# Two convolution tiles lead a mixer's GEMMs, its gates are woven in behind, and two gate tiles stand at the scan's end

## The chip, the cores and the metric

The kernel runs on one core of a Trainium2 chip. The metric is the time of one execution on the device in microseconds, median over the runs. The engines are TensorE (PE: matmuls, and its weight loads), VectorE (DVE), ScalarE (ACT), GpSimd (POOL) and SyncE (SP), whose queue issues most of the transfers. All matmul results land in PSUM, of which the kernel uses eight banks of 128 x 512 fp32.

## The reference

512 tokens of width 1024 pass through two layers of a first kind and two of a second. Only the mixers of the first kind change. With h the normalised input:

```python
proj = h @ w_in[l]
(qa, ka, va, qd, kd, vd, beta_logit, decay_logit, z, gate_logit) = jnp.split(proj, offsets, axis=-1)
...
y_attn = grid_attention(qa, ka, va) @ w_o_attn[l]
qkv = jax.nn.silu(centred_depthwise_conv(jnp.concatenate([qd, kd, vd], axis=-1), dn_conv_w[l]))
...
o = bidir_gated_deltanet(qd, kd, vd, beta, g)
o = rmsnorm(o, dn_out_norm_g[l]) * jax.nn.silu(z)
y_dn = o @ w_o_dn[l]
gates = jax.nn.sigmoid(gate_logit).reshape(b, s, N_BRANCH, D_MODEL)
mixed = gates[:, :, 0] * y_attn + gates[:, :, 1] * y_dn
x = x + mixed @ w_out[l]
```

The delta net is a recurrence over chunks of 64 tokens, run in both directions; before its scan, a triangular system is solved per chunk. A feed-forward layer follows each mixer.

## The kernel before, in words

Activations lie feature by token, as tiles of 128 features x 512 tokens. Every operand of a GEMM is split into a high and a low part (`xh`, `xl` and, per weight tile, `wh`, `wl`), and three matmuls per pair of tiles give fp32 accuracy. `wload` (L390) loads a 256 KB piece of weights, ACT rounds it to `wh`, and DVE subtracts to give `wl`; a running sum `aid` sends some of these subtractions to POOL instead. `g_fm` (L414) makes one output tile of 128 features from 1024 inputs: 24 matmuls of 512 columns in two pieces of weights, then an `evac` function on the result. Its output takes one of three PSUM banks `pg`.

The norm's factor per token, `R`, is applied to the results of the GEMMs and not to their inputs. So GEMMs can start before the norm is known: `lead` (L177) runs the first 16 steps of a mixer's GEMM on the inputs while the norm is worked out, and `follow` (L195) later runs what is left of these generators, that is their `evac`. Every `evac` here waits for `R`.

The mixer (L1325) has four sorts of work.

- The **delta net's preparation** (`prepare`, L1280): the gates (`g_dn_gates`, L864: a GEMM of 32 columns, then softplus, cumulative sums on PE, a trip through DRAM of sixteen small transfers on SP), the q, k and v projections with their convolution (`g_dn_inputs`, L947, twice, once per group of four heads, six tiles each), and the decay factors (`g_dn_decay`). Beside them run the grid attention's inputs (`g_grid_inputs`, L772). The `evac` of a convolution tile (L956) is a chain: DVE multiplies by `R` into `pad`, ACT and DVE apply five taps into `cva`, ACT and DVE make the silu, PE transposes four times into a `pt` bank, ACT copies out and squares, DVE reduces. At the end `rsqrt` steps give `dnr`, and DVE scales `tmk` and `tmq`, the keys and queries that the solve takes.
- The **solve** (`g_dn_solve`, L1012), a row by row elimination on DVE for two groups.
- The **scan** (`g_dn_scan`, L1111) of the two groups, with the grid attention beside it.
- **Background tiles** (`g_tanh`, L1254): four silu gates `z`, eight branch gates `ga` for the attention, eight branch gates `gd` for the delta net. Each is 24 matmuls; its `evac` is a DVE step into `tha`, a tanh on ACT into `thz`, for `z` one more DVE step, and a store to DRAM.

The work is woven by rates: `weave` (L219) always advances the generator that is furthest behind, and `run` pulls the background at a rate `R1[...]` per unit of foreground. `need` (L172) runs what is left of a name. A manual dependency in `pe` (L240) holds each background matmul behind the foreground instruction `pin` places back in the list of the last ones. From the program order the tile framework makes each engine's instruction order; every engine then works through its own in order.

After the scan come the output GEMM of the attention (results in `pg`, its `evac` into `u`), the norm of the delta net's output (`g_dn_out`), its GEMM, and the residual.

Of the kernel before, what the change touches and what calls it, by code (L numbers as in the profile page):

```python
# [11 lines left out]
AF = mybir.ActivationFunctionType  # L12
ALU = mybir.AluOpType
AX = mybir.AxisListType
# [5 lines left out]
T = 512  # L20
D = 1024
NT = 4
# [84 lines left out]
class Net:  # L107
# [839 lines left out]
    def g_dn_inputs(self, l, pool, ip, g):  # L947

        w = self.I["w_in"][l]
        out = {}  # L950
        ms = self.t(self.sm, [128, 2, NT, 4], "dnms")
        for kind in range(3):
            dst = self.t(pool, [128, NT, 256], "tm" + "qkv"[kind], bufs=2)
            out["qkv"[kind]] = dst

            def evac(i, ps, kind=kind, dst=dst):  # L956
                ft = 4 * kind + 2 * g + i
                c = [self.cols[:, 64 + 60 * l + 12 * j + ft : 65 + 60 * l + 12 * j + ft] for j in range(5)]
                p = self.pad[self.npad % 2]
                self.npad += 1  # L960
                self.tt(p[:, 2 : T + 2], ps, self.R, ALU.mult)
                a = self.t(ip, [128, T], "cva")
                self.act(a, p[:, 2 : T + 2], AF.Copy, scale=c[2])
                for j in (0, 1, 3, 4):
                    self.stt(a, p[:, j : j + T], c[j], a, ALU.mult, ALU.add)
                th = self.t(ip, [128, T], "cvt")
                self.act(th, a, AF.Tanh, scale=0.5)
                self.stt(a, th, 1.0, a, ALU.add, ALU.mult)
                pt = self.t(self.pt, [128, T], "pt")
                for t in range(NT):  # L970
                    self.tr(pt[:, 128 * t : 128 * t + 128], a[:, 128 * t : 128 * t + 128])
                p3 = pt.rearrange("p (t n) -> p t n", t=NT)
                self.act(dst[:, :, 128 * i : 128 * i + 128], p3, AF.Copy, scale=0.5 if kind == 2 else 1.0)
                if kind < 2:
                    sq = self.t(ip, [128, T], "cvt")
                    self.act(sq, pt, AF.Square)
                    self.V.tensor_reduce(ms[:, kind, :, 2 * i : 2 * i + 2],
                                         sq.rearrange("p (t h d) -> p t h d", t=NT, h=2), AX.X, ALU.add)

            yield from self.g_fm(w, D, 768 + 512 * kind + 256 * g, 256, self.xh, self.xl, evac, 128)  # L980
# [291 lines left out]
    def delta_net(self, l, od, inputs, attention):  # L1272
# [5 lines left out]
        ip, icm = self.pool(f"dni{l}", bufs=4)  # L1278

        def prepare():  # L1280
            G = yield from self.g_dn_gates(l, pool, ep, ip)
            x0 = yield from self.g_dn_inputs(l, pool, ip, 0)
            x1, E0, E1 = yield from self.weave(
                (self.g_dn_inputs(l, pool, ip, 1), 1.0), (self.g_dn_decay(l, ep, 0, G), R1[0]),
                (self.g_dn_decay(l, ep, 1, G), R1[0]),
            )
            return G, (x0, x1), (E0, E1)
# [31 lines left out]
    def begin_mixer(self, l):  # L1319
        self.zd = self.t(self.dr, [128, 4, T], f"zd{l}")  # L1320
        z = self.tanh_tiles(self.I["w_in"][l], 2336, 4, lambda f: self.zd[:, f, :], True)
        self.push("z", *z[2:])
        return [(g, 8) for g in z[:2]]

    def mixer(self, l):  # L1325
# [12 lines left out]
        self.follow()  # L1338
        self.push("ga", *self.tanh_tiles(w, 2848, 8, lambda f: thd[:, f, :]))
        self.push("gd", *self.tanh_tiles(w, 2848 + 1024, 8, lambda f: thd[:, 8 + f, :]))  # L1340
# [8 lines left out]
        for name in ("z", "ga", "gd"):  # L1349
            self.need(name)  # L1350
        pool, cm = self.pool(f"mo{l}", bufs=2)
# [607 lines left out]
```

## Time and profile before

| | |
|---|---|
| median of 3 runs | 3095.34 us (3093.31 to 3095.86) |
| the profiled execution | 3096.09 us, span 3094.3 us |
| PE busy | 3011.5 us, 97% |
| DVE busy | 2221.3 us, 72% |
| ACT busy | 1502.0 us, 49% |
| POOL busy | 416.4 us, 13% |
| granted PE clock, mean | 0.988 |

The span runs from the first to the last instruction of one execution. The busy share of an engine is an average over stages; for the change the two mixers count, of which layer 0's fills the span up to about 450 us and layer 1's stands from about 905 to 1310 us. The granted clock is 1 at full speed (2.4 GHz) and 0.5 at half (1.2 GHz); a stretch with a value between has run part of its time at either. The duration of a matmul in the trace contains its pipeline, so how fast PE works is read from the starts of neighbouring matmuls.

### The profile page before, as it was taken

The page shows a single profiled execution, that of the slowest core. Times are in us where ns is not written, and L with a number is a line of the kernel's source. Part 1 is how long each engine was busy: PE and PEld are TensorE (multiplying, and loading weights), DVE is VectorE, ACT ScalarE, POOL GpSimd, SP SyncE. Part 2 cuts the span into 40 slices and gives each one's busy share as a digit, 9 for nine tenths or more (in the row PEclk, how much of TensorE's full clock was granted, in tenths as well). Part 3 has the DMA queues.
Part 4 walks back from the last instruction along what each step waited for, and adds up shares of the span by engine and source line. Part 5 has one row for each costly group of instructions (what it writes and reads, how often), then busy time and mean ns, then how long its engine had stood idle before and what let it go on. Part 6 is the DMA issues. An engine that isn't in the chain of part 4 may idle for free. (4 is left out here: it accounts for less than half of the span.)

```text
span 3094.3 us, 54458 instructions
## 1 busy us (share of the span) xinstructions
PE 3011.5 (97%) x20148; PEld 2540.6 (82%) x20148; DVE 2221.3 (72%) x4974; ACT 1502.0 (49%) x3043; POOL 416.4 (13%) x550
## 2 busy tenths in 40 slices
PE   8989999999999899999999999999999999999999
PEld 6877778888888777788888898888888898878977
DVE  5988776777448887777774466778686666788684
ACT  3544744444324456544443344366464453476463
POOL 2433300000014343100000000200100010200200
PEclk9999999999999999999999999999999999999999
DMA  4435125333343342253333454522435545422525
GB/s 146 115 90 146 43 88 175 96 99 96 125 129 89 106 120 85 68 167 107 98 98 123 136 140 131 143 75 73 123 113 186 158 118 150 121 66 67 162 87 183
DMA packets 403116, 359.02 MB, mean 116 GB/s; under 512 B 32867, under 2 KB 350307, under 8 KB 402851
## 3 DMA queue, kind: packets, MB, share of 16 engines
q1 hardware_dynamic: 396707, 335.62, 37.6%
q0 software_dynamic: 6144, 19.93, 1.8%
q8 instruction: 159, 2.61, 0.4%
q14 instruction: 106, 0.87, 0.1%
HBM read 293.98 MB, written 61.47 MB: 115 GB/s over the span
## 5 line engine op out<-in xcount | busy, mean ns | idle before, releaser
L260 ACT ACTIVATE wh<-st 128x512 fp32r<-128x512 f32 x844 | 528.2, 629 | 788.5 <-PE pg L238 633.4
L254 DVE TENSOR_TENSOR wl<-st,wh 128x512 fp32r<-128x512 f32 x766 | 539.0, 705 | 402.0 <-ACT wh L260 397.2
L238 PE MATMUL pg<-xh,wh 128*128 128x512 f32 (+1 forms) x1824 | 733.0, 402 | 3.6 <-ACT wh L260 2.2
L238 PE MATMUL pg<-xh,wl 128*128 128x512 f32 (+1 forms) x1824 | 719.9, 395 | 5.3 <-POOL wl L254 5.3
L238 PE MATMUL pg<-xl,wh 128*128 128x512 f32 (+1 forms) x1824 | 712.2, 395 | 0.0
L238 PEld LDWEIGHTS pg<-xl,wh 128*128 128x128 f32 (+1 forms) x1824 | 343.4, 188 | 73.8 <-issue 0.4
L238 PEld LDWEIGHTS pg<-xh,wl 128*128 128x128 f32 (+1 forms) x1824 | 344.2, 189 | 72.0 <-POOL wl L254 7.0
L238 PEld LDWEIGHTS pg<-xh,wh 128*128 128x128 f32 (+1 forms) x1824 | 344.2, 189 | 70.7 <-ACT wh L260 2.6
L238 PE MATMUL pg<-wl,xh 128*128 128x256 f32 x928 | 265.1, 287 | 0.4 <-DVE wl L254 0.4
L238 PE MATMUL pg<-wh,xh 128*128 128x256 f32 x928 | 262.6, 287 | 1.1 <-DVE oz L257 0.8
L238 PE MATMUL pg<-wh,xl 128*128 128x256 f32 x928 | 263.0, 285 | 0.0
L238 PEld LDWEIGHTS pg<-wh,xh 128*128 128x128 f32 x928 | 176.3, 192 | 6.2 <-DVE oz L257 1.0
L238 PEld LDWEIGHTS pg<-wl,xh 128*128 128x128 f32 x928 | 177.9, 192 | 3.9 <-DVE wl L254 0.8
L238 PEld LDWEIGHTS pg<-wh,xl 128*128 128x128 f32 x928 | 177.7, 192 | 1.2
L485 POOL DMA_DIRECT2D xd<-xn x40 | 21.8, 544 | 1049.5 <-DVE xn L257 927.5
L254 POOL TENSOR_TENSOR wl<-st,wh 128x512 fp32r<-128x512 f32 x78 | 123.1, 1584 | 267.5 <-ACT wh L260 234.4
L238 PE MATMUL pg<-hh,wl 128*128 128x512 f32 x352 | 137.0, 389 | 0.0
L238 PE MATMUL pg<-hh,wh 128*128 128x512 f32 x352 | 136.7, 389 | 0.0
L238 PE MATMUL pg<-hl,wh 128*128 128x512 f32 x352 | 135.7, 389 | 0.0
L260 ACT ACTIVATE p<-pa,anb 128x128 f32<-128x128 f32 (+1 forms) x224 | 115.6, 517 | 36.9 <-DVE anb L725 34.0
L257 DVE SCALAR_TENSOR_TENSOR u<-pad,cols,u 128x512 f32<-128x512 f32 x176 | 127.3, 746 | 0.7
L260 ACT ACTIVATE ph<-pt 128x128 fp32r<-128x128 f32 (+1 forms) x224 | 94.9, 426 | 65.9 <-PE pt L251 64.5
(509 smaller groups left out, 6276.2 us busy)
## 6 DMA issues: line engine op xcount, KB each, us to landing
st<-in_w_in_dram SPq DMA_DIRECT2D x400, 256.0 KB
st<-in_w_up_dram SPq DMA_DIRECT2D x176, 256.0 KB
st<-in_w_down_dram SPq DMA_DIRECT2D x88, 256.0 KB
st<-in_w_out_dram SPq DMA_DIRECT2D x64, 256.0 KB
xo<-xd SPq DMA_DIRECT2D x48, 256.0 KB
th<-thz SPq DMA_DIRECT2D x48, 256.0 KB
xd<-xn POOLq DMA_DIRECT2D x40, 256.0 KB, 4.0
thd<-thz SPq DMA_DIRECT2D x32, 256.0 KB
```

What stands on the lines that cost most here:

```text
L238: return self.pe(self.PE.matmul(out, lhsT, rhs, start=start, stop=stop, **kw))
L254: return (eng or self.V).tensor_tensor(out, a, b, op)
L257: return self.V.scalar_tensor_tensor(out, a, s, b, op0, op1)
L260: return self.S.activation(out, in_, f, **kw)
L485: self.nc.gpsimd.dma_start(self.xd[:, k, :], x)
```

## The change

The convolution tile becomes a function of its own, `g_conv`. The two GEMM tiles that `lead` runs ahead of the norm are now the two q tiles of the first group (`begin_mixer`), and all four `z` tiles go to the background. `follow`, which finishes the led tiles, moves into `delta_net`, behind the opening of the pools that the convolution needs. In `prepare` the gates no longer come first: they are woven with the remaining four tiles of the first group (`led=2` leaves out the two that led). Two of the eight `gd` tiles are not pushed with the others but behind the scan, with `pin` at -12, which lets them stand among the last twelve foreground matmuls.

```diff
@@ -944,40 +944,51 @@
         self.act(gt, p4, AF.Exp)
         return beta3, fac, kds3, eg3, gt
 
-    def g_dn_inputs(self, l, pool, ip, g):
+    def g_conv(self, l, kind, f, dst, ms):
+        def evac(_, ps):
+            ft = 4 * kind + f
+            c = [self.cols[:, 64 + 60 * l + 12 * j + ft : 65 + 60 * l + 12 * j + ft] for j in range(5)]
+            p = self.pad[self.npad % 2]
+            self.npad += 1
+            self.tt(p[:, 2 : T + 2], ps, self.R, ALU.mult)
+            a = self.t(self.conv_pool, [128, T], "cva")
+            self.act(a, p[:, 2 : T + 2], AF.Copy, scale=c[2])
+            for j in (0, 1, 3, 4):
+                self.stt(a, p[:, j : j + T], c[j], a, ALU.mult, ALU.add)
+            th = self.t(self.conv_pool, [128, T], "cvt")
+            self.act(th, a, AF.Tanh, scale=0.5)
+            self.stt(a, th, 1.0, a, ALU.add, ALU.mult)
+            pt = self.t(self.pt, [128, T], "pt")
+            for t in range(NT):
+                self.tr(pt[:, 128 * t : 128 * t + 128], a[:, 128 * t : 128 * t + 128])
+            p3 = pt.rearrange("p (t n) -> p t n", t=NT)
+            i = f % 2
+            self.act(dst()[:, :, 128 * i : 128 * i + 128], p3, AF.Copy, scale=0.5 if kind == 2 else 1.0)
+            if kind < 2:
+                sq = self.t(self.conv_pool, [128, T], "cvt")
+                self.act(sq, pt, AF.Square)
+                self.V.tensor_reduce(ms()[:, kind, :, 2 * i : 2 * i + 2],
+                                     sq.rearrange("p (t h d) -> p t h d", t=NT, h=2), AX.X, ALU.add)
 
         w = self.I["w_in"][l]
-        out = {}
-        ms = self.t(self.sm, [128, 2, NT, 4], "dnms")
+        return self.g_fm(w, D, 768 + 512 * kind + 128 * f, 128, self.xh, self.xl, evac, 128)
+    def dn_tiles(self, pool, g):
+        x = {k: self.t(pool, [128, NT, 256], "tm" + k, bufs=2) for k in "qkv"}
+        return x, self.t(self.sm, [128, 2, NT, 4], "dnms")
+    def g_dn_inputs(self, l, g, tiles, led=0):
+        out, ms = tiles
         for kind in range(3):
-            dst = self.t(pool, [128, NT, 256], "tm" + "qkv"[kind], bufs=2)
-            out["qkv"[kind]] = dst
-
-            def evac(i, ps, kind=kind, dst=dst):
...
-            yield from self.g_fm(w, D, 768 + 512 * kind + 256 * g, 256, self.xh, self.xl, evac, 128)
+            for i in range(2):
+                if 2 * kind + i >= led:
+                    yield from self.g_conv(l, kind, 2 * g + i, lambda kind=kind: out["qkv"[kind]], lambda: ms)
         v = self.small(32, "dnv", 2)
         self.V.tensor_scalar(v, ms.rearrange("p a t h -> p (a t h)"), 4 * EPS, None, ALU.add)
         r = self.small(32, "dnr", 2)
@@ -1276,12 +1287,16 @@
         pool, cm = self.pool(f"dn{l}", bufs=2)
         ep, ecm = self.pool(f"dne{l}", bufs=4, side="right")
         ip, icm = self.pool(f"dni{l}", bufs=4)
+        self.conv_pool = ip
+        self.conv_tiles = self.dn_tiles(pool, 0)
+        self.follow()
 
         def prepare():
-            G = yield from self.g_dn_gates(l, pool, ep, ip)
-            x0 = yield from self.g_dn_inputs(l, pool, ip, 0)
+            x0, G = yield from self.weave(
+                (self.g_dn_inputs(l, 0, self.conv_tiles, 2), 1.0), (self.g_dn_gates(l, pool, ep, ip), 0.8)
+            )
             x1, E0, E1 = yield from self.weave(
-                (self.g_dn_inputs(l, pool, ip, 1), 1.0), (self.g_dn_decay(l, ep, 0, G), R1[0]),
+                (self.g_dn_inputs(l, 1, self.dn_tiles(pool, 1)), 1.0), (self.g_dn_decay(l, ep, 0, G), R1[0]),
                 (self.g_dn_decay(l, ep, 1, G), R1[0]),
             )
             return G, (x0, x1), (E0, E1)
@@ -1318,9 +1333,9 @@
 
     def begin_mixer(self, l):
         self.zd = self.t(self.dr, [128, 4, T], f"zd{l}")
-        z = self.tanh_tiles(self.I["w_in"][l], 2336, 4, lambda f: self.zd[:, f, :], True)
-        self.push("z", *z[2:])
-        return [(g, 8) for g in z[:2]]
+        self.push("z", *self.tanh_tiles(self.I["w_in"][l], 2336, 4, lambda f: self.zd[:, f, :], True))
+        lead = lambda i: self.g_conv(l, 0, i, lambda: self.conv_tiles[0]["q"], lambda: self.conv_tiles[1])
+        return [(lead(i), 8) for i in range(2)]
 
     def mixer(self, l):
         self.last = deque(self.last, maxlen=LAG[0])
@@ -1335,9 +1350,9 @@
         gp, gcm = self.pool(f"mix{l}", bufs=2)
         self.gp = gp
         od = [self.t(gp, [128, 2, T], f"o{g}", bufs=1) for g in range(2)]
-        self.follow()
         self.push("ga", *self.tanh_tiles(w, 2848, 8, lambda f: thd[:, f, :]))
-        self.push("gd", *self.tanh_tiles(w, 2848 + 1024, 8, lambda f: thd[:, 8 + f, :]))
+        gd = self.tanh_tiles(w, 2848 + 1024, 8, lambda f: thd[:, 8 + f, :])
+        self.push("gd", *gd[:6])
 
         def gate(f, ps, dst):
             th = self.t(dp, [128, T], "th", bufs=4)
@@ -1348,6 +1363,11 @@
         oa, hcm = self.delta_net(l, od, inputs, lambda pool, hp: self.g_grid_attention(l, pool, hp, qd, kd, vd, ad))
         for name in ("z", "ga", "gd"):
             self.need(name)
+        self.push("gd", *gd[6:])
+        self.pin = -12
+        self.need("gd")
+        self.pin = 0
         pool, cm = self.pool(f"mo{l}", bufs=2)
         mx = self.f32r_tiles(pool, NK, "m")
         dp, dcm = self.pool(f"md{l}", bufs=2)
```

How this moves instructions shows at two places. The first is DVE in layer 0 from the moment `R` is there. `tha`, `thz` are a gate tile's steps, `sq` (here) the result of the gates' GEMM, `beta`, `dnx`, `spe`, `spz` the softplus chain behind it, `pad` and `cva` a convolution's steps. Before:

```order
L257 SCALAR_TENSOR_TENSOR tha_389<-pg_274,R_376 128x512
L254 TENSOR_TENSOR sq_522<-pg_427,R_376 32x512
L257 SCALAR_TENSOR_TENSOR thz_391<-thz_391,tha_389 128x512
L257 SCALAR_TENSOR_TENSOR tha_395<-pg_311,R_376 128x512
L257 SCALAR_TENSOR_TENSOR thz_397<-thz_397,tha_395 128x512
L254 TENSOR_TENSOR wl_714<-st_712,wh_713 128x512
L880 TENSOR_SCALAR beta_528<-beta_528 128x64
L254 TENSOR_TENSOR dnx_531<-pa_420,r_dn_dt_bias_416 128x64
```

After the change the first eight rows, in front of these, are `pad` of the two led tiles (from `pg_274` and `pg_311`) and six of their taps:

```order
L257 SCALAR_TENSOR_TENSOR cva_403<-pad_5_98,cols_104,cva_403 128x512
L254 TENSOR_TENSOR wl_653<-st_651,wh_652 128x512
L257 SCALAR_TENSOR_TENSOR cva_422<-pad_6_99,cols_104,cva_422 128x512
L254 TENSOR_TENSOR pad_5_98<-pg_440,R_376 128x512
L257 SCALAR_TENSOR_TENSOR cva_403<-cvt_409,cva_403 128x512
L257 SCALAR_TENSOR_TENSOR cva_623<-pad_5_98,cols_104,cva_623 128x512 x4
L973 TENSOR_REDUCE dnms_401<-cvt_418 128x4x2
L257 SCALAR_TENSOR_TENSOR cva_422<-cvt_428,cva_422 128x512
L254 TENSOR_TENSOR sq_687<-pg_537,R_376 32x512
```

Before, the two silu tiles and the gates stand first, and the first `pad` comes seventeen rows behind the first row here; after the change two convolutions stand first, then a third, and the gates' `sq` comes sixteen rows behind the first.

The second is PE at the end of layer 0's scan. `po` is the grid attention's output, `qf`, `S`, `wt`, `qk`, `y` are operands of the scan, `ph` and `pl` next to weights are the attention's result as the input of the output GEMM, whose first tile is `pg_5459`; `xh` and `xl` are the mixer's input. Before:

```order
L238 MATMUL po_4628<-ph_4705,v_4152 128x256
L238 MATMUL po_4628<-pl_4706,v_4152 64x256
L238 MATMUL pg_5459<-ph_4861,wh_5461 128x512
L238 MATMUL pg_5459<-ph_4861,wl_5462 128x512
L238 MATMUL pg_5459<-pl_4863,wh_5461 128x512
```

After the change the first kept gate tile, `pg_5333`, begins among the scan's last products:

```order
L238 MATMUL pt_5230<-qk_2026,y_1002_5231 64x64 x4
L238 MATMUL pt_5229<-qk_2026,y_1002_5231 64x64 x4
L238 MATMUL pa_5248<-S_997_5192,wt_987_5112 64x64 x4
L238 MATMUL pg_5333<-xh_28_160,wh_5335 128x512
L238 MATMUL pg_5333<-xh_28_160,wl_5336 128x512
L238 MATMUL pg_5333<-xl_36_168,wh_5335 128x512
L238 MATMUL pg_5333<-xh_29_161,wh_5335 128x512
L238 MATMUL pa_5249<-qf_984_5092,S_997_5192 64x64 x4
L238 MATMUL pg_5333<-xh_29_161,wl_5336 128x512
```

and the second, `pg_5375`, ends right ahead of the output GEMM:

```order
L238 MATMUL pg_5375<-xl_42_174,wh_5395 128x512
L238 MATMUL pg_5375<-xh_35_167,wh_5395 128x512
L238 MATMUL pg_5375<-xh_35_167,wl_5396 128x512
L238 MATMUL pg_5375<-xl_43_175,wh_5395 128x512
L238 MATMUL pg_5459<-ph_4777,wh_5461 128x512
L238 MATMUL pg_5459<-ph_4777,wl_5462 128x512
```

Before, the output GEMM follows the last product of the attention at once; after the change 48 matmuls of the two kept tiles stand between, the first 16 of them woven with products of the scan.

## Rows read from the trace of the kernel before

**Rows 1.** The page, part 1: busy time, share of the span, instructions.
```profile
span 3094.3 us, 54458 instructions
...
PE 3011.5 (97%) x20148; PEld 2540.6 (82%) x20148; DVE 2221.3 (72%) x4974; ACT 1502.0 (49%) x3043; POOL 416.4 (13%) x550
```

**Rows 2.** Busy time by stretch, layer 0 and then layer 1, from R on.
```profile
core 0: us, PE busy (x) PEld busy (x) DVE busy (x) ACT busy (x) POOL busy (x), PEclk, DMA share, GB/s
45.60:60.00 14.40, 13.74 (x77) 12.32 (x78) 10.99 (x25) 4.04 (x8) 2.59 (x2) 0.88 0.30 92
60.00:75.00 15.00, 15.00 (x126) 12.51 (x125) 7.77 (x15) 4.92 (x9) 1.72 (x1) 0.89 0.23 58
75.00:185.00 110.00, 108.22 (x613) 89.46 (x610) 102.85 (x200) 53.44 (x96) 53.48 (x44) 1.00 0.37 102
185.00:200.60 15.60, 8.84 (x41) 7.50 (x42) 14.41 (x28) 8.69 (x16) 4.40 (x6) 0.67 0.38 125
sum 155.00, PE 145.79 PEld 121.80 DVE 136.01 ACT 71.09 POOL 62.18; mean PE 36.45 PEld 30.45 DVE 34.00 ACT 17.77 POOL 15.54
...
920.00:937.00 17.00, 17.00 (x154) 14.59 (x153) 9.76 (x19) 4.51 (x10) 1.29 (x1) 0.90 0.26 67
937.00:1052.00 115.00, 110.96 (x608) 91.68 (x606) 102.44 (x202) 56.33 (x99) 52.47 (x45) 1.00 0.37 102
...
sum 160.00, PE 150.00 PEld 125.01 DVE 134.32 ACT 72.90 POOL 59.94; mean PE 37.50 PEld 31.25 DVE 33.58 ACT 18.23 POOL 14.98
```

**Rows 3.** Groups of DVE instructions by form, 45.6 to 200.6 us.
```profile
L257 DVE SCALAR_TENSOR_TENSOR cva<-pad,cols,cva 128x512 f32<-128x512 f32 x48 | 39.8, 832 | 2.2 <-ACT cva L260 1.6
L254 DVE TENSOR_TENSOR wl<-st,wh 128x512 fp32r<-128x512 f32 x22 | 17.1, 782 | 3.8 <-ACT wh L260 3.7
...
L257 DVE SCALAR_TENSOR_TENSOR thz<-thz,tha 128x512 f32<-128x512 f32 x4 | 3.8, 958 | 0.8 <-ACT thz L260 0.7
...
L257 DVE SCALAR_TENSOR_TENSOR tha<-pg,R 128x512 f32<-128x512 f32 x4 | 2.8, 688 | 2.0 <-ACT R L260 1.7 <-PE pg L238 0.2
```

**Rows 4.** PE in order of time, both preparations' ends: start, duration, instruction, [idle before].
```profile
189.18 1.09 PE L251 MATMUL pt<-c_ident,cva 128*128 128x128 f32 x4 [4.89 <-DVE hl L254]
192.85 1.09 PE L251 MATMUL pt<-c_ident,cva 128*128 128x128 f32 x4 [2.59 <-DVE dnv L982]
...
1055.38 1.09 PE L251 MATMUL pt<-c_ident,cva 128*128 128x128 f32 x4 [4.73 <-DVE hl L254]
1059.05 1.09 PE L251 MATMUL pt<-c_ident,cva 128*128 128x128 f32 x4 [2.58 <-DVE dnv L982]
```

**Rows 5.** PE in order of time at the scan's end, both layers.
```profile
433.11 0.79 PE L238 MATMUL pg<-ph,wh 128*128 128x512 f32 x1 [3.90 <-ACT ph L260]
433.70 0.63 PE L238 MATMUL pg<-ph,wl 128*128 128x512 f32 x1
434.13 0.63 PE L238 MATMUL pg<-pl,wh 128*128 128x512 f32 x1
...
446.22 0.40 PE L238 MATMUL pg<-ph,wl 128*128 128x512 f32 x1
446.45 0.40 PE L238 MATMUL pg<-pl,wh 128*128 128x512 f32 x1
...
1297.23 0.80 PE L238 MATMUL pg<-ph,wh 128*128 128x512 f32 x1 [3.79 <-ACT ph L260]
```

**Rows 6.** Busy time by stretch, after the scan in layer 0 (columns as rows 2).
```profile
433.10:446.00 12.90, 12.89 (x54) 10.82 (x55) 5.61 (x21) 3.63 (x6) 0.53 (x1) 0.64 0.73 224
```

**Rows 7.** GpSimd and DVE in order of time, layer 0; then page, part 5.
```profile
170.13 3.79 POOL L254 TENSOR_TENSOR wl<-st,wh 128x512 fp32r<-128x512 f32 x2 [6.62 <-ACT wh L260]
...
170.82 1.29 DVE L254 TENSOR_TENSOR nw<-nwb 128x16 f32<-128x16 f32 x1
...
L257 DVE SCALAR_TENSOR_TENSOR u<-pad,cols,u 128x512 f32<-128x512 f32 x176 | 127.3, 746 | 0.7
```

More of the change, by code (lines that the diff above doesn't have):

```diff
@@ L945, in g_dn_gates @@
         return beta3, fac, kds3, eg3, gt
-    def g_dn_inputs(self, l, pool, ip, g):
-        w = self.I["w_in"][l]
-        out = {}
-        ms = self.t(self.sm, [128, 2, NT, 4], "dnms")
-        for kind in range(3):
-            dst = self.t(pool, [128, NT, 256], "tm" + "qkv"[kind], bufs=2)
-            out["qkv"[kind]] = dst
-            def evac(i, ps, kind=kind, dst=dst):
[L957 to L978, printed above, removed]
-            yield from self.g_fm(w, D, 768 + 512 * kind + 256 * g, 256, self.xh, self.xl, evac, 128)
```

## The prediction

> **What bounds the kernel now.** The page's first part [rows 1] comes first: TensorE (PE) is busy 3011.5 of 3094.3 us, so a change that adds and removes no matmul can only win PE's idle time, about 83 us, and what is lost while its clock is granted at half. The page's slices put most of that idle time outside the start into the two mixers, so I cut the first half of each mixer into stretches [rows 2]: from the moment R is ready (45.6 us in layer 0, 906.9 us in layer 1) to the end of the scaled q and k tiles that the solve needs (200.6 and 1066.9 us). I call that the preparation; it takes 155.0 and 160.0 us. VectorE (DVE) is busy 136.0 us of the first and 134.3 us of the second, PE 145.8 and 150.0 us. So both are nearly full, and not at the same time: early on DVE is starved (busy for 7.8 of 15.0 us from 60 to 75 us, for 9.8 of 17.0 us from 920 to 937 us) while PE works; in the middle both run; at the end DVE is full (14.4 of 15.6 us) and PE works for only 8.8 of 15.6 us.
>
> The end is where it shows on PE [rows 4]: the transposes of the last convolution tiles wait 4.89 and 2.59 us in layer 0, 4.73 us and again 2.6 us in layer 1. The releasers are DVE instructions: a queue of convolution steps comes due when no matmul is left to cover it.
>
> The second place is the scan's end [rows 5]: PE stands 3.90 us (layer 0) and 3.79 us (layer 1) before the first matmul of the attention's output GEMM, and that GEMM then starts at the lower clock: neighbouring matmuls begin 0.43 us apart (433.70, 434.13) where they are 0.23 us apart later (446.22, 446.45). The granted clock from 433.1 to 446.0 us is 0.64 on average [rows 6].
>
> **What moves.** The two silu-gate tiles that led each mixer's GEMMs (24 matmuls of 512 columns each) become background tiles; two tiles of the q convolution lead instead; two branch-gate tiles leave the background and stand at the scan's end. So the background keeps its number of tiles, and per mixer 48 matmuls leave the preparation and turn up at the scan's end: 48 x 0.233 us = 11.2 us at full clock [rows 5]. No matmul is added or dropped.
>
> **Term 1, preparation.** On PE it loses 11.2 us. On DVE less: convolution tiles are still finished after R, since they need it, so all twelve convolutions remain (48 multiply-adds, [rows 3]). What goes, counted in the two orders between R and the scaled q, is two tha steps (0.688 us), two thz steps (0.958 us) and three weight splits (0.782 us): 1.4 + 1.9 + 2.3 = 5.6 us.
>
> The other gain on DVE is order. Now the gates' small GEMM and its chain of small DVE steps go first, and the first convolution reaches DVE only after them; that is the starved stretch. After the change two finished convolution tiles lie ready the moment R is, and the gates are woven in behind, as the first order excerpt shows. Two bounds follow. The upper one: only the 5.6 us go and all waits stay: 149.4 and 154.4 us. The lower one: no waits at all. DVE then needs 136.0 - 5.6 = 130.4 and 134.3 - 5.6 = 128.7 us. PE needs its busy time, less what half clock cost in it (1.7 us from 45.6 to 60 us and 1.6 us from 60 to 75 us by the granted 0.88 and 0.89, and at most 1.8 us at the end, where 10.3 us ran at half and PE stood for 6.8 of them; in layer 1 1.7 us by the 0.90 and again 1.8 us), less 11.2 us: 129.5 and 135.3 us. The lower bounds are therefore 130.4 us (DVE) and 135.3 us (PE). Between them I take each layer's own middle stretch as the nearest row, since there DVE is supplied and still shares with the other engines: 102.85 of 110.0 us and 102.44 of 115.0 us [rows 2], 0.935 and 0.891. At that fill the preparation takes 130.4 / 0.935 = 139.5 and 128.7 / 0.891 = 144.4 us: 15.5 and 15.6 us shorter, 31.1 us together (bounds 11.2 and 49.3).
>
> **Term 2, scan's end.** The 48 matmuls cost 22.4 us in two layers. They fill the waits of 3.90 and 3.79 us. If they keep the clock up, twelve matmuls of the first output tile and eight of the next get 0.19 us each back: 3.8 us per layer. So 22.4 - 7.7 - 7.6 = +7.1 us; with the clock not recovered +14.7 us. What their weight splits and tanh add on ScalarE and DVE lies beside 11.2 us of matmuls; without that cover it would be two splits and a tha step per tile, some 2.3 us. The loads on SP for the output GEMM are queued behind one store of a gate tile each, and the GEMM starts 11.2 us later, so I cost them at nothing.
>
> By the Trainium skill (TensorE: Matmul & The Clock Gate, Terms) the penalty of throttled time is that time multiplied by the part of the clock withheld. From the granted 0.64 over 12.9 us that is 9.3 us at half, 4.6 us lost; the rows give 3.8 us, because the small matmuls in between [rows 6] hardly ran slower, and I keep 3.8 us. By the page the sum would be 1.6 us better.
>
> **Term 3, solve.** Two silu tiles now fall into the solve instead of the preparation and the lead. Each has one thz step more than a branch-gate tile (0.958 us): 1.9 us per layer on a DVE whose row chain paces the solve, 3.8 us in all if nothing hides it, 0 if DVE's gaps do. I take 3.8 us. PE waits there for weight splits on GpSimd may come elsewhere; I give them 3 us of either sign.
>
> **Sum.** -31.1 + 7.1 + 3.8 = -20.2 us. The profiled execution took 3096.1 us (1.8 us around its span), so 3075.9 us; the median of the runs lies 0.75 us lower, so I predict 3075 us. A measurement of this kernel can tell about 0.2% from no change, 6.2 us.
>
> **Rivals.** *DVE saves only its own work.* The waits only change places: DVE's present waits are partly on ScalarE, and a fuller queue in order waits there too. Then the preparation gives 11.2 us, and the sum is -11.2 + 7.1 + 3.8 = -0.3 us: 3095 us, no change. For it: nothing in the profile forbids that PE simply stands for the 149.4 - 129.5 = 19.9 us. Against it: the 7.2 us of starvation per layer in one stretch have a named cause, which the new order removes. 0.14.
>
> *Both engines close up.* The preparation reaches its lower bounds: -49.3 + 7.1 + 0 = -42.2 us, 3053 us; anything past -33 us counts here. For it: DVE is filled to 14.4 of 15.6 us where it has a queue [rows 2]. Against it: chains through ScalarE. 0.12.
>
> *DVE and GpSimd collide more (the slow side).* The convolution's multiply-add takes 0.832 us here [rows 3] against 0.746 us for the like instruction in the feed-forward layer, where GpSimd is nearly idle, and a 16-column step took 1.29 us while GpSimd split weights [rows 7]. So sharing costs 48 x 0.086 = 4.1 us per layer today. If DVE without gaps meets GpSimd twice as often, 4.1 us per layer come on top of the first rival: -0.3 + 8.2 = +7.9 us, 3103 us. It decides from the point where the multiply-add's mean passes about 0.90 us with DVE's waits unchanged. Against it: in the order GpSimd's weight splits do not grow in number (78 before, 75 now, in the whole program). 0.07.
>
> The Trainium skill (SBUF — State Buffer, SBUF: two separate sides) calls the port pair an exclusive lock: of a GpSimd instruction and a DVE one with two SBUF inputs, the later waits for the whole of the earlier. The trace agrees with that as far as the 1.29 us beside a 3.79 us pair of GpSimd splits goes [rows 7]; by that rule every added wait would be a whole GpSimd instruction, which is the price rise this rival needs.
>
> *The change does not do what it says.* The scheduler could have sunk the kept tiles into the scan; the order excerpt shows them at its end, so this has 0.02.
>
> **Chances and range.** The forecast, to within 13 us of its sum, has 0.65. Faster by over 0.2%: the forecast, the closed-up case, and a third of the first rival that stops short: 0.65 + 0.12 + 0.04 = 0.81. Within 0.2%: the rest of the first rival and the last one: 0.12. Slower: 0.07. The low end lets the nearer part of the closed-up case in (-35 us, 3060 us); the high end takes the preparation two thirds of the way to its upper bound with half of the clock's part not recovered, -17.8 + 10.9 + 3.8 = -3.1 us: 3092 us. Some 0.2 is left out, most of it above.
>
> **What would show it.** Right: DVE busy above 0.9 from R on, with no starved stretch behind it; a preparation of 139 to 145 us; no wait above 1 us on the transposes of cva; no gap before the output GEMM and a granted clock near 1.0 there; two tiles of 24 matmuls ahead of it. Wrong: a preparation of 150 us or more with PE waiting on pad or cva; a multiply-add mean near 0.9 us; a new PE wait on fac or on weights while SP works through the gates' small transfers; a gap at the output GEMM that has only moved behind the kept tiles.

## The result, and the profile after

The changed kernel takes 3119.4 us (median of 4 runs, 3118.0 to 3125.6) against 3095.6 us (3093.3 to 3096.1) of the kernel before in the same comparison: ratio 1.0082, interval 1.0065 to 1.010. It is slower by 24 us; 20 us faster was forecast. The page's first part after, against [rows 1]:

```profile
span 3116.8 us, 54445 instructions
...
PE 3018.2 (97%) x20148; PEld 2547.1 (82%) x20148; DVE 2212.7 (71%) x4977; ACT 1503.9 (48%) x3043; POOL 404.3 (13%) x547
```

The span grew by 22.5 us. DVE lost 8.6 us of work; PE, with the same 20148 matmuls, was busy 6.7 us longer and idle the rest. Where that happened is seen when the mixer is cut at five places: R ready, the end of the scaled q, the solve's first row step, the scan's start (the end of the solve's last transpose), the first matmul of the attention's output GEMM. Layer 0 of the kernel before, by stretch (columns as in rows 2):

```profile
45.50:200.60 155.10, 145.79 (x847) 121.80 (x848) 136.10 (x266) 71.09 (x128) 62.18 (x53) 0.94 0.35 99
200.60:221.50 20.90, 20.90 (x320) 17.37 (x319) 14.07 (x23) 9.61 (x15) 3.74 (x3) 1.00 0.28 72
221.50:282.30 60.80, 55.72 (x360) 44.95 (x359) 59.62 (x141) 26.87 (x43) 27.08 (x18) 0.97 0.43 117
282.30:433.10 150.80, 144.76 (x2267) 115.82 (x2265) 107.91 (x280) 97.16 (x223) 39.57 (x71) 0.99 0.23 69
```

The same of the changed kernel, with the kept tiles as a stretch of their own, then layer 1's preparation and the sum of its five stretches (before: 390.3 us):

```profile
44.20:185.50 141.30, 129.76 (x785) 106.77 (x785) 124.00 (x256) 64.70 (x116) 49.66 (x46) 0.97 0.33 93
185.50:213.30 27.80, 26.18 (x337) 21.93 (x338) 16.59 (x27) 11.99 (x19) 4.63 (x6) 0.89 0.25 77
213.30:275.50 62.20, 56.04 (x358) 44.66 (x357) 61.59 (x141) 26.79 (x43) 31.51 (x19) 0.97 0.41 112
275.50:426.20 150.70, 143.42 (x2242) 116.16 (x2240) 104.62 (x268) 98.82 (x224) 40.17 (x71) 0.99 0.23 68
426.20:442.30 16.10, 16.10 (x84) 12.39 (x82) 6.97 (x20) 3.68 (x6) 0.53 (x1) 0.79 0.40 116
...
914.80:1057.00 142.20, 133.48 (x814) 110.66 (x812) 124.72 (x258) 64.98 (x118) 50.68 (x47) 0.98 0.35 97
...
sum 401.30, PE 377.85 PEld 308.49 DVE 312.49 ACT 206.56 POOL 127.14; mean PE 75.57 PEld 61.70 DVE 62.50 ACT 41.31 POOL 25.43
```

The preparation came out as forecast, 141.3 us (and 142.2 us in layer 1). The stretch behind it, which the sum had left alone, grew from 20.9 to 27.8 us (21.5 to 28.1 in layer 1; its granted clock fell from 1.00 to 0.89 in layer 0, as an estimate up to 27.8 x 0.11 = 3.1 us of that), the solve by 1.4 us (0.4), and scan and kept tiles together from 150.8 to 166.8 us (148.9 to 170.6). Over the mixer's first half that is +10.5 and +11.0 us: nearly all of the loss.

What left the preparation is matmuls. One of the three kinds of product of its 512-column GEMM, before and after, in the groups of instructions by form from R to the scaled q:

```profile
L238 PE MATMUL pg<-xh,wh 128*128 128x512 f32 x120 | 48.6, 407 | 1.4 <-DVE tha L257 1.4
```
```profile
L238 PE MATMUL pg<-xh,wh 128*128 128x512 f32 x90 | 36.7, 408 | 1.8 <-DVE dng L254 1.7
```

All such matmuls, the gates' few included, are 359 before and 294 after (367 and 308 in layer 1). 65 times 0.233 us [rows 5] is 15.1 us, and the stretch got 13.8 us shorter: in layer 0 the waits did not shrink at all. In layer 1, 59 matmuls are 13.7 us and the stretch got 17.7 us shorter, so some waiting went there. The starved stretch from 60 to 75 us did fill up (DVE 7.77 us of it in [rows 2], 12.60 us now), but starving moved behind it, and the end is as it was:

```profile
44.20:60.00 15.80, 14.13 (x90) 10.89 (x91) 13.81 (x18) 6.09 (x10) 3.48 (x2) 1.00 0.26 68
60.00:75.00 15.00, 14.86 (x82) 11.84 (x81) 12.60 (x38) 7.09 (x16) 2.02 (x2) 1.00 0.26 70
75.00:100.00 25.00, 23.31 (x192) 20.13 (x191) 17.43 (x44) 8.73 (x17) 9.25 (x12) 0.93 0.32 81
100.00:170.00 70.00, 70.00 (x396) 58.43 (x394) 65.94 (x125) 37.61 (x66) 29.62 (x25) 1.00 0.39 114
170.00:185.50 15.50, 7.46 (x34) 5.48 (x32) 14.22 (x34) 5.17 (x9) 5.29 (x6) 0.86 0.26 67
```

At the end PE waits as in [rows 4], in order of time, with one row of DVE behind it:

```profile
173.72 0.66 PE L251 MATMUL pt<-c_ident,cva 128*128 128x128 f32 x4 [3.42 <-DVE cva L257]
183.61 1.12 PE L251 MATMUL pa<-c_ident,tmk 128*128 128x128 f32 x8 [3.86 <-DVE tmk L254]
187.12 1.09 PE L251 MATMUL pt<-c_ident,cva 128*128 128x128 f32 x4 [2.38 <-DVE hl L254]
...
196.99 0.69 DVE L257 SCALAR_TENSOR_TENSOR BB<-pt,e 128x512 f32<-128x512 f32 x1 [9.40 <-PE pt L238]
```

The hl steps belong to the attention's inputs, whose last eight transposes (of the queries, qb) now stand behind all but four of the convolutions' transposes of cva; DVE then idles 9.40 us before the solve's first product, where in the kernel before its longest idle time there was 2.32 us.

At the scan's end the gap of [rows 5] is gone, and the low clock is not: it begins with the kept tiles and comes back in the output GEMM. PE in order of time:

```profile
425.17 0.50 PE L238 MATMUL pt<-qf,S 64*64 64x64 f32 x5 [1.32 <-DVE y L254]
426.24 0.50 PE L238 MATMUL pg<-xh,wh 128*128 128x512 f32 x1
...
429.36 0.63 PE L238 MATMUL pg<-xl,wh 128*128 128x512 f32 x1
429.79 0.63 PE L238 MATMUL pg<-xh,wh 128*128 128x512 f32 x1
...
436.12 0.39 PE L238 MATMUL pg<-xh,wh 128*128 128x512 f32 x1
436.35 0.39 PE L238 MATMUL pg<-xh,wl 128*128 128x512 f32 x1
...
447.96 1.86 PE L238 MATMUL pt<-c_ident,sq 128*128 128x2 f32 x8 [1.05 <-ACT sq L260]
451.39 0.78 PE L238 MATMUL pg<-ph,wh 128*128 128x512 f32 x1
451.97 0.63 PE L238 MATMUL pg<-ph,wl 128*128 128x512 f32 x1
```

From 429.4 to 433.6 us neighbours begin 0.43 us apart, later 0.23 us; the first 12.9 us of the output GEMM then have a granted clock of 0.74, against 0.64 in [rows 6].

### The profile page after: what moved, and what is told of

Same layout as the page of the kernel before. It is cut to its first block, busy times and chain, and to the rows that moved or that the text cites. A ratio compares the mean times of both kernels' runs of the same rounds, so it can differ in the third digit from the quotient of the medians.

```text
span 3116.8 us, 54445 instructions
## 1 busy us (share of the span) xinstructions
PE 3018.2 (97%) x20148; PEld 2547.1 (82%) x20148; DVE 2212.7 (71%) x4977; ACT 1503.9 (48%) x3043; POOL 404.3 (13%) x547
## 5 line engine op out<-in xcount | busy, mean ns | idle before, releaser
L254 POOL TENSOR_TENSOR wl<-st,wh 128x512 fp32r<-128x512 f32 (+1 forms) x75 | 119.6, 1602 | 236.5 <-ACT wh L260 226.3
L238 PE MATMUL po<-ph,v 128*128 128x256 f32 x480 | 125.0, 288 | 2.1 <-ACT ph L260 2.1
```

The lines of the kernel that those rows point to most:

```text
L238: return self.pe(self.PE.matmul(out, lhsT, rhs, start=start, stop=stop, **kw))
L254: return (eng or self.V).tensor_tensor(out, a, b, op)
```

## The experiments

Fifteen kernels were run. This table is what they come down to: the median and ratio of each (interval in brackets), and of its profiled execution, layer 0 and layer 1, the time from R to the solve's first step with the number of 512-column matmuls in it, and the time from the scan's start to the output GEMM with theirs (kept tiles included).

| kernel | median us | ratio | R to solve, us / matmuls | scan to output GEMM |
|---|---|---|---|---|
| before | 3095 | 1 | 176.0/401, 181.4/411 | 150.8/89, 148.9/84 |
| after | 3119.4 | 1.0082 | 169.1/347, 170.3/363 | 166.8/145, 170.6/145 |
| hold_only | 3108.1 | 1.0042 [1.0027, 1.0057] | 175.9/401, 180.8/411 | 159.5/89, 154.1/88 |
| lead_only | 3121.7 | 1.0085 [1.007, 1.01] | 164.1/347, 170.4/357 | 167.8/144, 169.7/145 |
| lead_weave | 3127.5 | 1.0104 [1.0085, 1.0123] | 167.8/347, 169.4/361 | 168.1/145, 171.8/139 |
| lead_hold | 3111.2 | 1.0048 [1.0031, 1.0064] | 166.0/347, 175.4/357 | 164.9/145, 166.6/142 |
| weave_only | 3104.3 | 1.0029 [1.0017, 1.0041] | 180.2/401, 185.7/415 | 149.9/89, 149.8/84 |
| lead_back | 3106.4 | 1.0034 [1.0021, 1.0047] | 180.0/401, 181.5/411 | 151.4/89, 150.9/89 |
| lead_spread | 3105.3 | 1.0033 [1.0018, 1.0047] | 164.3/359, 170.9/369 | 162.1/128, 164.1/128 |
| two_taps | 3100.5 | 1.0019 [1.0008, 1.0029] | 160.8/347, 165.7/361 | 166.8/147, 169.1/142 |
| after_in | 3106.9 | 1.0043 [1.0027, 1.006] | 168.3/363, 167.0/363 | 166.1/147, 162.3/139 |
| lead_hold_in | 3108.4 | 1.0043 [1.0028, 1.0058] | 163.7/347, 169.5/357 | 165.8/146, 165.5/139 |
| spread_in | 3109.6 | 1.0044 [1.0029, 1.0059] | 164.4/362, 172.6/374 | 162.8/129, 161.6/128 |
| lead_back_in | 3091.6 | 0.9987 [0.9978, 0.9997] | 171.0/401, 176.7/411 | 151.0/89, 150.6/88 |
| weave_back_in | 3096.3 | 1.0007 [0.9998, 1.0016] | 173.4/413, 181.6/415 | 151.0/89, 149.6/89 |
| after_back_in | 3127.7 | 1.0103 [1.0088, 1.0118] | 173.9/413, 180.8/415 | 163.3/89, 158.7/88 |
| lead_back_in7 | 3094.9 | 1.0006 [0.9996, 1.0015] | 173.4/401, 177.1/411 | 151.1/89, 150.0/89 |

Stretches of kernels whose order is the same there repeat to some 0.6 us up to the solve (before and hold_only: 176.0 and 175.9, 181.4 and 180.8). Each stretch is from one profiled execution.

**The three parts apart.** hold_only is the kernel before with two gate tiles kept (the diff's last two hunks, `follow` staying where it was); lead_only the changed kernel without them and without the weave; lead_weave leaves out the kept tiles alone, lead_hold the weave alone. Of lead_only:

```diff
-            x0, G = yield from self.weave(
-                (self.g_dn_inputs(l, 0, self.conv_tiles, 2), 1.0), (self.g_dn_gates(l, pool, ep, ip), 0.8)
-            )
+            G = yield from self.g_dn_gates(l, pool, ep, ip)
+            x0 = yield from self.g_dn_inputs(l, 0, self.conv_tiles, 2)
...
-        self.push("gd", *gd[:6])
+        self.push("gd", *gd)
```

> The kernel before with one part of the change: two branch gate tiles per mixer leave the background and stand at the scan's end. Theory A (keeping the tiles is what costs: matmuls that would have covered a wait stand where they cover one gap of 3.9 us and run at a low clock): slower by 8 to 20 us, 3104 to 3116 us; the kept tiles take about 16 us per layer as in the changed kernel, and waits of PE in solve and scan grow. Theory B (the silu tiles that join the background, with their longer chain on DVE, cost it): no change, 3091 to 3099 us. Theory C (the woven gates cost it, by coming later): no change, 3091 to 3099 us.

> The changed kernel with its two other parts undone: two q convolution tiles lead, the gates stand first in the preparation as before, and all eight branch gate tiles are background, so that 22 tiles are. Theory A: no change, 3090 to 3101 us, the preparation shorter by about what its matmuls take and the rest longer by the same. Theory B: slower, 3106 us or more. Theory C: no change, 3090 to 3101 us.

> The changed kernel with nothing kept for the scan's end: convolutions lead, gates woven, 22 background tiles. Theory A: 3090 to 3104 us, 15 us or more below the changed kernel. Theories B and C: within 8 us of the changed kernel, 3111 us or more.

> The changed kernel with the gates first again: convolutions lead, two tiles are kept. Theory A: as the changed kernel, 3110 to 3125 us. Theory B: the same. Theory C: no change against the kernel before, 3090 to 3101 us, and the stretch from the scaled q and k tiles to the solve's first step back from 27.8 to about 21 us.

Theory A was right about hold_only (+12.5 us) and wrong about the rest: the lead alone costs 26 us, the most of any part, and with the lead keeping tiles even helps (lead_only to lead_hold, -10.5 us; the profiled executions have 7.2 us of it from layer 0's output GEMM to the feed-forward layer's R). B named the lead, but for a reason that does not show: the solve grew by 1.4 us only. C fails: without the weave the stretch behind the preparation is still 28.1 us.

hold_only shows what the last two background tiles were for. Busy time by stretch from the scan's start, before and then hold_only:

```profile
282.30:302.30 20.00, 20.00 (x449) 16.00 (x448) 10.52 (x21) 12.58 (x22) 6.00 (x7) 0.92 0.67 179
302.30:322.30 20.00, 20.00 (x220) 15.23 (x219) 11.45 (x25) 12.83 (x31) 4.18 (x8) 1.00 0.39 128
```
```profile
281.60:301.60 20.00, 17.17 (x454) 13.08 (x453) 11.20 (x22) 12.29 (x22) 4.77 (x6) 0.93 0.63 181
301.60:321.60 20.00, 18.57 (x157) 14.10 (x158) 7.79 (x18) 9.39 (x23) 4.05 (x8) 0.50 0.14 46
```

Without them the background ends within the scan's first 20 us, the granted clock falls to 0.50 for the next 20 us, and PE does 157 matmuls there in place of 220. The background's tail lay beside the scan's start, not beside its end.

**Place or kind.** lead_back raises the rate at which the preparation draws background (`R1[4]`, 0.059 to 0.17), lead_spread that of the solve (`R1[1]`, 0.633 to 0.75), both on lead_only; weave_only weaves the gates in the kernel before; two_taps cuts DVE work in the changed kernel by leaving out two of the four multiply-adds of each convolution. Of lead_back, then of two_taps:

```diff
-R1 = [2.071, 0.633, 0.45, 3.49, 0.059, 9.505, 0.491, 4.55, 0.469, 0.387, 0.519, 0.788]
+R1 = [2.071, 0.633, 0.45, 3.49, 0.17, 9.505, 0.491, 4.55, 0.469, 0.387, 0.519, 0.788]
...
-            for j in (0, 1, 3, 4):
+            for j in (1, 3):
```

> Lead only (convolutions lead, gates first, nothing kept), and the rate at which the preparation draws background raised from 0.059 to 0.17, so that each stage of the mixer holds as many 512-column matmuls in program order as in the kernel before (417 up to the solve, 276, 90, and 9 at the scan's end). Theory D (the matmuls that leave the preparation only move, and cost where they pile up at the scan's end): 3088 to 3100 us, no change against before, the preparation about 155 us again, no surplus at the scan's end. Theory E (the new lead costs by itself: silu tiles in the solve, the backlog of convolution on DVE): 3108 us or more, as lead only. Theory F (the first forecast: order on DVE closes the preparation's waits, and was only given back elsewhere): below 3086 us.

> Lead only, and the rate of background in the solve raised from 0.633 to 0.75: the preparation stays short (369), and solve and scan take the surplus earlier, so that 7 matmuls instead of 60 are left for the scan's end. Theory D, if it is the end that is dear and not the moved work itself: 10 to 20 us below lead only, 3102 to 3112 us. Theory E: as lead only, 3117 us or more, since the solve on DVE gets longer with every tile in it.

> The kernel before with only the gates woven beside the first convolutions, which have no lead here. Theory D: no change, 3091 to 3100 us, with the starved stretch of DVE 60 to 75 us filled and the wait for DVE at the preparation's end as long as before. Theory F: faster by over 6 us, since the starved stretch was time lost. Weaving by itself costing something (lead with weave was 5.8 us above lead alone): 3100 to 3104 us.

> The changed kernel with two of the four multiply-adds of each convolution left out (taps 0 and 4), which takes 24 x 0.80 = 19 us per layer from DVE and nothing from PE. If DVE's own work paces the preparation: the stretch from R to the solve's first step, 169 us in layer 0, gets shorter by 10 us or more per layer, PE's waits on tmk, hl and cva at its end go, and the sum is 20 to 40 us less. If chains through ScalarE and PSUM pace it, as the rival of unchanged waits has it: less than 5 us per layer.

Place is most of it: with the matmuls back in the preparation the scan is 151.4 and 150.9 us again, and 15 of lead_only's 26 us are gone. But D had said no change, and 11 us stay, 4.0 us of them ahead of the solve in layer 0.

lead_spread is 16 us below lead_only. Its scan is 5.7 and 5.6 us shorter with 16 and 17 matmuls fewer in it (3.7 and 4.0 us), and from the output GEMM to the feed-forward layer's R it wins 4.4 and 1.3 us. The expectation put the surplus at the scan's end; on PE it does not lie there. The last background matmul of lead_only's layer 0 begins 57.4 us after the scan's start at 271.7 us (28.7 us in the kernel before, 38.9 us in lead_spread), and scan and output GEMM read:

```profile
329.11 0.48 PE L238 MATMUL pg<-xl,wh 128*128 128x512 f32 x1
...
271.70:439.50 167.80, 160.51 (x2323) 125.12 (x2321) 110.98 (x281) 101.99 (x230) 39.70 (x71) 1.00 0.23 71
439.50:456.60 17.10, 16.17 (x54) 13.81 (x55) 7.32 (x27) 3.60 (x6) 0.53 (x1) 0.51 0.63 196
```

So the scan is the dear place, and not its end: 55 more matmuls (12.8 us) make it 17.0 us longer at a granted clock of 1.00, with PE busy 15.7 us longer. Why they cost more than their time there is open; behind the scan the output GEMM then runs at 0.51.

weave_only contradicts the forecast by itself: weaving the gates makes the way to the solve 4.2 and 4.3 us longer, not shorter. two_taps splits the waits. By stretch, R to the scaled q and on to the solve, and PE's largest wait in the second:

```profile
44.60:170.80 126.20, 125.40 (x773) 104.28 (x773) 97.28 (x225) 60.18 (x109) 44.24 (x43) 0.99 0.34 96
170.80:205.40 34.60, 27.82 (x349) 23.08 (x350) 23.38 (x34) 16.04 (x26) 8.99 (x10) 0.90 0.31 92
...
PE pt L251 <- DVE hl L254: 6.3, 1, 6.3
```

With 19 us less on DVE PE stands for 0.8 us in the first stretch (11.5 us in the changed kernel): DVE does pace it. But the second grows to 34.6 us, with a wait of 6.3 us for the attention's inputs, so only 8.3 and 4.6 us of 19 arrive. The inputs are a second thing that ends late. That is so for a kernel with half of its taps; in the changed kernel itself PE waits 2.38 us for hl.

**Where the inputs end.** The attention's inputs are woven beside the preparation at a share of it (`R1[6]`, 0.491). The lead took two convolutions out of the preparation and left the share, so the inputs' end slid back: in PE's order of the kernel before, their last eight transposes stand ahead of the last twelve cva transposes, in the changed kernel behind all but the last four. A share of 0.6 puts them ahead of the last twelve again:

```diff
-R1 = [2.071, 0.633, 0.45, 3.49, 0.059, 9.505, 0.491, 4.55, 0.469, 0.387, 0.519, 0.788]
+R1 = [2.071, 0.633, 0.45, 3.49, 0.059, 9.505, 0.6, 4.55, 0.469, 0.387, 0.519, 0.788]
```

> The changed kernel with one number changed: the share at which the attention's inputs are woven beside the preparation, 0.491 to 0.6, so that their last eight transposes stand ahead of the last twelve cva transposes in PE's order, as in the kernel before, and not behind all but one of these groups. Theory H (the preparation got shorter for its own work only; the attention's inputs, woven at an unchanged share, came out behind it, and PE and DVE wait for them with nothing left to cover it): the wait of the solve's first DVE steps (9.4 us in layer 0) goes, from R to the solve's first step 160 to 165 us instead of 169.1, and 3103 to 3112 us in all. Rival (what paces that stretch is DVE's own backlog of convolution, wherever the inputs stand): 3115 us or more.

> Lead and kept tiles, gates first, and the inputs' share at 0.6. Theory H: 5 to 10 us below lead with kept tiles (3111 us), 3100 to 3106 us, and about 8 us below the run that weaves the gates as well. Rival of the backlog: 3109 us or more.

> Lead only with the background drawn faster in the solve (0.75) and the inputs' share at 0.6: the best arrangement by theories D and H together, a version meant to beat both kernels. D and H: 3093 to 3101 us. Rival of the backlog: as without the inputs' share, 3102 us or more.

> Lead only with the background's rate in the preparation at 0.17 (each stage with as many matmuls as before) and the inputs' share at 0.6 (the same order at the preparation's end): what is left is the order alone, with two finished convolution tiles at R instead of two gate tiles. Theory F (the first forecast's reason): below 3088 us. Theory H with D: 3092 to 3101 us, the 3.7 us that the stretch behind the preparation had grown by are gone. Rival of the backlog: as without the inputs' share, 3103 us or more.

lead_back_in is what H and D expected, to half a us (F's 3088 us was not reached), 14.8 us below lead_back by one number, and the only version faster than the kernel before (by 0.03 to 0.22%, where 0.2% was taken as the least that can be told). In the other three the share does less: spread_in gained nothing, as H's rival had it, lead_hold_in 2.8 us, inside the interval and between the two, and of after_in's 12.5 us only 0.8 and 3.3 us lie ahead of the solve, where H wanted 4 to 9. Its layer 1 scan is 8.3 us shorter. Scan with kept tiles, the changed kernel's layers 0 and 1, then after_in's layer 1, then layer 1 of the kernel before:

```profile
275.50:442.30 166.80, 159.52 (x2323) 128.54 (x2322) 111.59 (x287) 102.50 (x230) 40.71 (x72) 0.97 0.25 72
1145.50:1316.10 170.60, 161.75 (x2323) 130.33 (x2322) 111.78 (x287) 102.72 (x230) 39.81 (x72) 0.96 0.25 71
...
1142.00:1304.40 162.40, 154.58 (x2318) 124.60 (x2317) 111.62 (x288) 102.33 (x230) 39.80 (x72) 1.00 0.24 72
...
1148.30:1297.20 148.90, 142.29 (x2261) 114.19 (x2260) 108.77 (x280) 96.75 (x223) 38.30 (x70) 1.00 0.23 71
```

As an estimate from these rows, up to 170.6 x 0.04 = 6.8 us of the 8.3 us are clock; six matmuls fewer in after_in (139 for 145) are 1.4 us. Whether the clock goes with the order or with the one execution that was profiled is not shown.

The pair lead_back_in and lead_hold_in prices the place. They differ in the background's rate in the preparation and in the two kept tiles, so 48 of the matmuls that reach the scan's stretch stand behind the scan. First lead_back_in, then lead_hold_in, layer 0, R to the scaled q, to the solve, and the scan with what follows up to the output GEMM:

```profile
44.50:196.10 151.60, 145.21 (x858) 121.85 (x859) 130.85 (x267) 72.85 (x130) 60.48 (x54) 0.97 0.36 104
196.10:215.50 19.40, 19.40 (x310) 15.99 (x308) 13.90 (x22) 8.77 (x14) 2.45 (x2) 1.00 0.26 69
...
276.40:427.40 151.00, 144.82 (x2267) 115.88 (x2265) 107.92 (x280) 97.19 (x223) 39.57 (x71) 0.99 0.22 68
```
```profile
44.60:185.10 140.50, 129.97 (x778) 109.42 (x779) 128.17 (x259) 66.33 (x121) 53.39 (x48) 0.94 0.34 98
185.10:208.30 23.20, 23.20 (x334) 19.39 (x334) 15.21 (x23) 10.73 (x16) 4.74 (x5) 1.00 0.26 70
...
270.50:436.40 165.90, 158.62 (x2334) 127.91 (x2325) 111.81 (x288) 102.72 (x230) 40.67 (x72) 0.98 0.24 73
```

In both layers 54 matmuls (12.6 us at 0.233 us) leave the way to the solve, which gets 7.3 and 7.2 us shorter, and the scan's stretch grows by 14.8 and 14.9 us. So 12.6 us of matmuls cost little more than half their time in the preparation, where PE would stand for DVE without them, and more than their time in and behind the scan.

**Weave and kept tiles with nothing else moved.** Still open was what these two cost once both numbers are set back. weave_back_in is lead_weave, after_back_in the changed kernel, each with 0.17 and 0.6; lead_back_in7 has 0.7.

> Lead with both rates set back (0.17 and 0.6), and the gates woven at 0.8; nothing kept. If weaving costs by itself (the gates' small steps and the decay behind them come later, between large ones, on a DVE that has no gap for them): 5 to 9 us above the same kernel without it (3091.6 us), 3096 to 3101 us, lost in the preparation. If it only cost by moving the inputs: 3088 to 3094 us.

> The changed kernel, all three parts, with both rates set back (0.17 and 0.6). 48 matmuls then leave the background's end for the place behind the scan, as in the run that only keeps tiles. Cover theory (the background's last two tiles lay beside the scan's first 40 us, and without them TensorE's clock falls there): half clock for 10 to 20 us within the scan's first 40 us in both layers, and 8 to 14 us above the run without kept tiles, 3100 to 3112 us. If the place behind the scan is what costs: no half clock there, the stretch of the kept tiles at a low clock, and a like sum.

> Lead only, the background's rate in the preparation 0.17, and the inputs' share 0.7 in place of 0.6: their last transposes then come still earlier among the convolutions. If the wait on hl (2.7 us in layer 0) is what is left of the inputs: 3086 to 3090 us. If the preparation's end is now DVE's backlog of convolution alone: 3090 to 3095 us, no change against 0.6.

Weaving costs 4.7 us by the medians, just under what it was to cost by itself: 2.4 and 4.9 us ahead of the solve. In layer 0 twelve more matmuls (2.8 us) fall into that stretch, which can be all of it; in layer 1 it is four more (0.9 us), so there some 4 us are left for the weave. In after_back_in the cover theory's mark is there in both layers, a granted clock of 0.52 and 0.51 over 21 us from some 20 us into the scan on:

```profile
299.20:320.40 21.20, 19.91 (x156) 14.90 (x156) 8.13 (x19) 10.09 (x24) 4.00 (x8) 0.52 0.15 51
...
1176.90:1197.50 20.60, 19.38 (x168) 14.44 (x168) 8.55 (x20) 9.98 (x25) 4.04 (x8) 0.51 0.19 65
```

The size was missed: 31 us above weave_back_in instead of 8 to 14, of which the scan has 12.3 and 9.1 us; the rest lies in other stretches, and its cause is open. A share of 0.7 gives no more than 0.6, which speaks for DVE's backlog as what is left at the preparation's end.

## Why the prediction was wrong

**Term 1, the number near and the reason not.** Forecast -15.5 and -15.6 us, measured -13.8 and -17.7 us. The step that failed is "between them I take each layer's own middle stretch as the nearest row". In layer 0 DVE's fill did not rise to 0.935: it is 124.0 / 141.3 = 0.88, as it was (136.1 / 155.1). In layer 1 it rose from 0.84 (134.3 / 160.0) to 0.88 (124.7 / 142.2); 0.891 was assumed. That the time still came out is luck: ahead of the marker DVE lost 12.1 and 9.6 us of work and not 5.6 us, and PE 65 and 59 matmuls and not 48. Eleven of these per layer had only passed the marker: between the scaled q and the solve's first step stand 53 and 55 in place of 42 and 44. So the marker was badly chosen: the scaled q came earlier, and what stands behind it, the end of the attention's inputs and the way to the solve, did not come earlier by as much. To the solve's first step it is -6.9 and -11.1 us, in layer 0 near the bound "only the 5.6 us go and all waits stay", in layer 1 midway to the forecast.

[rows 4] had shown the inputs: the releaser of the 4.89 and 4.73 us is hl, a step of theirs. I read it as "a queue of convolution steps", and the sum has no term for where the inputs end.

The order gain itself exists: with background and inputs where they were, lead_back_in is 5.0 and 4.7 us shorter up to the solve than the kernel before. I had put it at 31.1 - 22.4 = 8.7 us for both layers. It is the lead that gives it; by the medians only some 3 us of it reach the end of the kernel. The weaving of the gates, which I had counted as its other half, costs: the starved stretch was filled, and a new one stands behind it (17.43 of 25.0 us).

**Term 2, far too small.** I forecast +7.1 us for both layers, and scan with kept tiles grew by 16.0 and 21.7 us. "They fill the waits of 3.90 and 3.79 us" held. The step that failed is "If they keep the clock up": the clock is low in the kept tiles, where ten steps from one kept matmul to the next are 0.43 us long, 10 x 0.20 = 2.0 us, and low again in the output GEMM (0.74), and no gain shows where 3.8 us per layer were to come back: from its first matmul to the feed-forward layer's R it took 111.9 and 111.6 us before and 111.6 and 113.3 us after. The sign that I had named, "a gap at the output GEMM that has only moved behind the kept tiles", did not come, since PE waits 1.05 us at most there in layer 0; the low clock came without it. Eight and thirteen more background matmuls (1.9 and 3.0 us) fell into the scan before the kept tiles.

The granted clock prices the rest in part. Over scan and kept tiles it is 0.97 and 0.96, against 0.99 and 1.00 before: as an estimate from these rows up to 5.0 - 1.5 = 3.5 us more are lost in layer 0 and 6.8 us in layer 1. So 11.2 + 1.9 + 3.5 - 3.9 = 12.7 of the 16.0 us and 11.2 + 3.0 + 6.8 - 3.8 = 17.2 of the 21.7 us have a row. The remaining 3.3 and 4.5 us are not settled.

By the Trainium skill (TensorE: Matmul & The Clock Gate, Terms) the penalty is throttled time times the share withheld; as an estimate, the kept tiles' 16.1 us at 0.79 lose 16.1 x 0.21 = 3.4 us. The ten steps show 2.0 us of that; what the scan's matmuls between them lost is not read from a row.

**Term 3** was +3.8 us; the solve grew by 1.4 and 0.4 us, 1.8 us together.

**What the sum did not have.** It priced each part where it left and where it arrived, but not that a stage in which PE waits for DVE gives back less than the PE work that leaves it, and that the scan takes more than the work that arrives. Up to the solve 102 matmuls left in both layers (23.8 us at 0.233 us), and 18.0 us came off; from the scan's start to the output GEMM 117 arrived (27.3 us) and cost 37.7 us. The first rival said the former ("the waits only change places") and gave -11.2 us; measured up to the solve are -18.0 us. It came nearest to the mechanism, and ended at no change because it took over term 2. The slow rival had the side and not the cause: the multiply-add got faster, not slower (832 ns in [rows 3]):

```profile
L257 DVE SCALAR_TENSOR_TENSOR cva<-pad,cols,cva 128x512 f32<-128x512 f32 x48 | 37.4, 800 | 3.9 <-ACT cva L260 3.5
```

Together: -18.0 us up to the solve, +1.8 us in it, +37.7 us from the scan's start to the output GEMM, and about 1 us elsewhere make the span's 22.5 us. Against the sum of -20.2 us that is 42.7 us, of which term 2 has 30.6 us and term 1, taken up to the solve, 13.1 us; term 3 gives 2.0 us back.

## What to carry to other kernels

Work without dependences is worth what it covers: before moving it, ask what PE would do in its place, and price it at both ends; here 54 matmuls were worth 7 us in one stage, and in another the stretch that took them up grew by 15 us. In an order that weaves streams at fixed shares, taking work out of one stream moves the end of every other: after such a change, look up in the new order where each stream ends, and measure a stage to a point that all of them have passed. A rate and a share had to be set again together before a gain of the lead could be seen at all: 3 us, just clear of the noise.

## What was not expected of the hardware

A busy PE can be at half its speed for long: in hold_only it is busy 18.57 of 20.00 us by the profile and runs at a granted clock of 0.50, 1.2 in place of 2.4 GHz, right after a stretch in which it was busy 17.17 of 20.00 us, mostly with small matmuls (32 columns). Busy share alone would have shown 1.4 us lost there. The count of matmuls shows more: 157 for 220 in the kernel before, of which 26 are background that hold_only does not have there. And in the changed kernel the clock fell with the first kept matmuls, was back at the sixteenth, and fell again 14 us later in the output GEMM, though PE waited no more than 1.05 us between.
